# Group norms of a state-space mixer applied to the output products, with two dense tiles and three others moved in the order

## The chip, the cores and the metric

The kernel runs on one core of one Trainium2 chip. The core has a matrix engine (TensorE, PE in the profile; PEld is its weight load), a vector engine (VectorE, DVE), an activation engine (ScalarE, ACT), a general engine (GpSimd, POOL) and a queue engine (SyncE, SP) that issues most transfers. The metric is the device time of one execution in microseconds. Three runs of the kernel before took 1381.81, 1380.92 and 1374.41 us; their median, 1380.92 us, is what the change is measured against.

## What is computed

The reference is one inference step of one decoder layer, for 512 prompt tokens and 64 sampled ones (8 sequences of 8), 576 tokens in all, with a model width of 1024. Everything is fp32.

```
proj = rmsnorm(h) @ w_in                      # columns: z, xbc, dt, rwkv
A: xs, B, C = silu(conv4(xbc));  y = SSD(xs, dt, B, C) + d_skip * xs      # 16 heads x 64, 2 groups
   yg = y * silu(z)
   yg = yg * rsqrt(mean(yg * yg over the 512 channels of a group) + eps)  # per token and group
   y_ssd = yg * ssd_norm
B: y_rwkv = gate * (head_norm(rwkv7(...)) + bonus)                        # 16 heads x 64
h = h + concat(y_ssd, y_rwkv) @ w_out
h = h + (silu(f @ w_gate) * (f @ w_up)) @ w_down,   f = rmsnorm(h, norm_ffn)
h = h + sigmoid(rmsnorm(h) @ w_ple_gate) * (p @ w_ple_proj)
y = rmsnorm(h)
```

The grouped norm has one factor for each token and group of 512 channels. It multiplies a whole column of yg, so it can be applied ahead of the output product, or to that group's share of the product. `ssd_norm` is one factor for each channel and cannot be moved in this way.

## The kernel before

**Layout.** Activations lie transposed, channels on the 128 partitions and the 576 tokens along the row, so a 1024-wide activation is 8 tiles. Each fp32 product is made of three products of halves (hi·hi, hi·lo, lo·hi): `mm3` (L211 to L215) issues them for two stretches of 288 tokens, so one tile of 128 input channels by 128 output channels is 6 matmuls, and `linear` (L217) makes an output tile from a list of input tiles; with 8 input tiles that is 48 matmuls. The weights are streamed: `wsplit` (L189) loads 128x512 of them on SP's queue (raw), makes the high half on ACT (whi, L92 is the one line of all `act` calls) and the low half in turn on POOL and DVE (wlo, L198). `split` (L177, L186) does the same for activations. An output tile lies in PSUM (`lin`, two buffers, until the feed-forward stage opens two more).

**Stages.** Input projections and four quarters of the RWKV mixer come first. A quarter is `prep` (keys bk are made at L560 and L561), `gram` (key-query products by groups of windows, L589, masks at L599), `solve` (triangular inverses by many small DVE operations, L650 and L652), `combine` (L674, L688), `chain` (the serial pass over windows, L765 to L823) and `head_norm` (L875 to L889). Between their steps stand dense tiles from a list: projections of a quarter, convolution tiles (L352, taps at L371, L376 and L377) and gate tiles `zed` (L380), which make silu(z) and park it in memory. The table FP says how many tiles of the list go behind each step of `prep` (entries 0 to 4) and of `gram` (entry 5 behind the first group, 6 behind the third).

After the fourth quarter's chain is written, the string SEQ interleaves what is left: 's' is a step of the state-space generator `ssd` (L968), 'z' a gate tile, 'p' the input-embedding products (`ple_proj`, L947; parked as pp), 'y' loads and splits the first six RWKV result tiles (YR), and 'w' makes the share of those six in the first output tile and parks it (part_d).

The state-space part makes transposes (L1061), chunk states (L1074), eight sampled sequences (L1122) and eight prompt tiles (`prompt`, L1143; its last products are L1170 and L1177, the skip term L1178, the share of earlier chunks L1179). `gated` (L1181) is called for group 0 after prompt tile 5 and for group 1 after tile 7. It multiplies each of four xs tiles by silu(z) (L1190, z read back from memory), adds the squares of the four tiles (ACT, and three additions on POOL, L1196), lets `rstd_by_token` (L302) sum them over channels (20 one-column matmuls, L310), take root and reciprocal (L313) and spread the factors over the partitions (L316), copies them to SBUF (bc), multiplies xs by `ssd_norm` and the factors (DVE, L1204), and splits the result into the halves y (low halves in turn on DVE and POOL, L186).

**Output product.** Seven output tiles take the eight RWKV tiles first (L1244 and after, `residual` adds x at L1261), and later the eight state-space tiles in 48 matmuls, added into h on DVE (L1295); the first tile takes the last two RWKV tiles and the eight state-space tiles in 60 matmuls. After each tile `after` scales h by `norm_ffn` (hg, L1274), splits it for the feed-forward stage (xhi, xlo), squares it and adds the squares up (L1279, mostly on POOL). The 22 feed-forward tiles follow, then `w_down` with the same `after` for the next norm, the embedding gate and the final norm.

**What sets the order.** The program is written in one order; a scheduler then places each engine's instructions by a simulated timeline, with the written order as priority. An instruction that is written later may thus stand earlier if its inputs are there. Each engine runs its own list strictly in order.

Of the kernel before, what the change touches and what calls it, by code (L numbers as in the profile page):

```python
# [8 lines left out]
F32 = mybir.dt.float32  # L9
F32R = mybir.dt.float32r  # L10
# [33 lines left out]
SEQ = "zzszszszspyw"  # L44
# [7 lines left out]
FP = ((1, 0, 1, 0, 1, 0, 0, 0), (1, 0, 1, 0, 1, 0, 0, 0), (1, 0, 1, 0, 1, 0, 0, 0), (0, 0, 0, 0, 0, 0, 0, 3))  # L52
# [22 lines left out]
def hybrid_step(ctx, tc, A):  # L75
# [226 lines left out]
    def rstd_by_token(acc, scale, a=0, b=NT, banks=None):  # L302
# [5 lines left out]
        for i, c in enumerate(ws):  # L308
            for h in (0, 64):
                T.matmul(st[h:h + 64, i:i + 1], acc[:, c + h:c + h + 64], ones[:, 0:1], start=True, stop=True)  # L310
# [657 lines left out]
    def ssd():  # L968
# [174 lines left out]
        def prompt(j):  # L1143
# [35 lines left out]
            G.tensor_tensor(xs[j][:, 192:NT], xs[j][:, 192:NT], er[:], ALU.add)  # L1179

        def gated(g):  # L1181

            qa = mt("bc", [P, NT], bufs=4)
            for i in range(4):
# [6 lines left out]
                if i == 0:  # L1191
                    act(qa[:], xs[j][:], AF.Square)
                else:
                    qb = mt("bc", [P, NT], bufs=4)
                    act(qb[:], xs[j][:], AF.Square)
                    G.tensor_tensor(qa[:], qa[:], qb[:], ALU.add)  # L1196
            std = mt("bc", [P, NT], bufs=4)
            banks = d_ps(), d_ps()
            rstd_by_token(qa, 1.0 / 512, banks=banks)
            act(std[:, 0:448], banks[0][:, 0:448])  # L1200
            act(std[:, 448:NT], banks[1][:, 0:128])
            for i in range(4):
                j = 4 * g + i
                V.scalar_tensor_tensor(xs[j][:], xs[j][:], par("ssd_norm", j), std[:], ALU.mult, ALU.mult)  # L1204
                y2 = k4("y2", [P, 2, NT], dt=F32R)
                split(xs[j][:], None, (None, None), None, lo_eng=(V, G)[i % 2], hi=y2[:, 0], lo=y2[:, 1])
                YS.append((y2[:, 0], y2[:, 1]))

# [11 lines left out]
    YS = []  # L1220
# [45 lines left out]
    for c in range(NPART, 8):  # L1266
        ps = lin_ps()
        linear(YR, ps)
        residual(c, ps, A["xT"][c])

    def after(c, h, gname, pool, tag, bufs, state):

        t = pool.tile([P, NT], F32, tag=tag, name=nm("hg"), bufs=bufs)
        V.tensor_scalar(t[:], h[:], par(gname, c), None, ALU.mult)  # L1274
        state["x"].append(split(t[:], xp, ("xhi", "xlo"), [P, NT]))
# [10 lines left out]

    st = {"x": []}
    for c in range(8):
        ps = lin_ps()
        if c < NPART:  # L1290
            linear(YR[6:8] + YS, ps)
            residual(c, ps, part_d[c][:])
        else:
            linear(YS, ps)
            V.tensor_tensor(hs[c][:], ps, hs[c][:], ALU.add)  # L1295
# [220 lines left out]
```

## Time and profile before

| what | value |
|---|---|
| median of three runs | 1380.92 us (1374.41 to 1381.81) |
| the profiled execution | 1375.24 us |
| its span, first to last instruction | 1373.5 us |
| outside the span | 1.74 us |
| mean granted clock of TensorE | 0.936 |
| PE busy | 1256.6 us (91%) |
| DVE, ACT, POOL busy | 717.5, 576.5, 553.6 us |
| DMA over the span | 97 GB/s |

The stages lie in the trace about as follows: input side and quarters one to three to 530 us, the solve of the fourth quarter 530 to 568, its combine and chain 568 to 672, its head norm 673 to 694, the state-space part 696 to 809, the rest of the output product to 879, then the feed-forward and the last stages.

An execution on the chip was recorded; a row of a timeline is one instruction or a run of like ones: start and duration in us, engine, line of the kernel, operation, output and inputs, shapes, how many, and in brackets the idle time of the engine ahead of it and what ended that. Matmuls overlap, so a matmul's own duration is longer than the distance to the next one, and the distance is its cost. A window's row sums each engine's busy time in a stretch. The granted clock is 1.00 at full speed and 0.50 at half.

### The profile page before, as it was taken

The page shows a single profiled execution, that of the slowest core. Times are in us where ns is not written, and L with a number is a line of the kernel's source. Part 1 is how long each engine was busy: PE and PEld are TensorE (multiplying, and loading weights), DVE is VectorE, ACT ScalarE, POOL GpSimd, SP SyncE. Part 2 cuts the span into 40 slices and gives each one's busy share as a digit, 9 for nine tenths or more (in the row PEclk, how much of TensorE's full clock was granted, in tenths as well). Part 3 has the DMA queues.
Part 4 walks back from the last instruction along what each step waited for, and adds up shares of the span by engine and source line. Part 5 has one row for each costly group of instructions (what it writes and reads, how often), then busy time and mean ns, then how long its engine had stood idle before and what let it go on. Part 6 is the DMA issues. An engine that isn't in the chain of part 4 may idle for free.

```text
span 1373.5 us, 26233 instructions
## 1 busy us (share of the span) xinstructions
PE 1256.6 (91%) x10525; PEld 1158.4 (84%) x10525; DVE 717.5 (52%) x1330; ACT 576.5 (42%) x1148; POOL 553.6 (40%) x547
## 2 busy tenths in 40 slices
PE   6897999999989979888969968999999999999995
PEld 5786897889868858767748858999999999999995
DVE  6648757797778777744365664322222222222265
ACT  6565346534562653433433354333233333222253
POOL 5326415632452253224355665433233233344442
PEclk9997999899979989879969988999999999999998
DMA  4322342234222313432625621322222222222342
GB/s 161 123 70 62 84 119 89 69 99 129 68 73 90 105 63 92 133 134 86 197 83 179 200 69 63 85 77 85 84 79 85 85 79 84 85 80 81 115 133 70
DMA packets 94458, 135.56 MB, mean 99 GB/s; under 512 B 34704, under 2 KB 39056, under 8 KB 94336
## 3 DMA queue, kind: packets, MB, share of 16 engines
q1 hardware_dynamic: 94336, 133.88, 32.0%
q8 instruction: 83, 1.36, 0.4%
q14 instruction: 39, 0.32, 0.1%
HBM read 106.10 MB, written 27.75 MB: 97 GB/s over the span
## 4 chain that ended last, share of the span: by engine, by line
PE 42%; DVE 6%; ACT 2%; DMA 2%; POOL 1%; issue 1%; DVEq 0%; SPq 0%; ACTq 0%; POOLq 0%
PE lin L213 13%; PE lin L215 13%; PE lin L214 13%; DMA raw<-wts 1%; DVE pg L1364 1%; PE d L1127 1%; DVE h L1365 1%; PE d L1139 1%; PE y L1177 0%; DVE xs L1204 0%; DMA yl<-yr_d 0%; ACT sq L92 0%; DVE h L1382 0%; DVE xs L1190 0%; DVE wp L198 0%
## 5 line engine op out<-in xcount | busy, mean ns | idle before, releaser
L213 PE MATMUL lin<-xhi,whi 128*128 128x288 f32 (+1 forms) x1488 | 450.1, 303 | 3.7 <-ACT whi L92 2.2
L215 PE MATMUL lin<-xhi,wlo 128*128 128x288 f32 (+1 forms) x1488 | 447.3, 301 | 2.3 <-POOL wlo L198 2.3
L214 PE MATMUL lin<-xlo,whi 128*128 128x288 f32 (+1 forms) x1488 | 447.4, 301 | 0.6 <-POOL xlo L186 0.6
L198 POOL TENSOR_TENSOR wlo<-raw,whi 128x512 fp32r<-128x512 f32 (+1 forms) x136 | 180.5, 1327 | 490.0 <-ACT whi L92 465.3
L92 ACT ACTIVATE whi<-raw 128x512 fp32r<-128x512 f32 (+1 forms) x272 | 169.0, 621 | 410.1 <-PE lin L214 344.9
L213 PEld LDWEIGHTS lin<-xhi,whi 128*128 128x128 f32 (+1 forms) x1488 | 281.3, 189 | 10.8 <-issue 2.6
L215 PEld LDWEIGHTS lin<-xhi,wlo 128*128 128x128 f32 (+1 forms) x1488 | 281.9, 189 | 8.2 <-POOL wlo L198 3.0
L214 PEld LDWEIGHTS lin<-xlo,whi 128*128 128x128 f32 (+1 forms) x1488 | 281.5, 189 | 5.3 <-issue 1.5
L198 DVE TENSOR_TENSOR wlo<-raw,whi 128x512 fp32r<-128x512 f32 (+1 forms) x136 | 97.1, 714 | 171.8 <-ACT whi L92 169.1
L213 PE MATMUL lin<-ah,whi 128*128 128x288 f32 x352 | 104.1, 296 | 0.0
L215 PE MATMUL lin<-ah,wlo 128*128 128x288 f32 x352 | 103.8, 295 | 0.3
L214 PE MATMUL lin<-al,whi 128*128 128x288 f32 x352 | 103.8, 295 | 0.0
L215 PEld LDWEIGHTS lin<-ah,wlo 128*128 128x128 f32 x352 | 66.3, 188 | 1.0 <-POOL wlo L198 1.0
L214 PEld LDWEIGHTS lin<-al,whi 128*128 128x128 f32 x352 | 66.1, 188 | 0.0
L213 PEld LDWEIGHTS lin<-ah,whi 128*128 128x128 f32 x352 | 66.0, 187 | 0.0
L1323 DVE TENSOR_TENSOR sg<-lin,sg 128x576 f32<-128x576 f32 x22 | 16.7, 758 | 83.2 <-PE lin L215 81.9
L650 DVE TENSOR_TENSOR tmp<-L,Tt 72x30 f32<-72x30 f32 (+14 forms) x120 | 51.6, 430 | 3.2
L1318 DVE TENSOR_TENSOR sg<-lin,rstd 128x576 f32<-128x576 f32 x22 | 16.6, 757 | 68.8 <-PE lin L215 68.7
L213 PE MATMUL lin<-xu,whi 128*128 128x288 f32 x128 | 39.9, 313 | 8.8 <-ACT xu L92 7.1
L215 PE MATMUL lin<-xu,wlo 128*128 128x288 f32 x128 | 39.9, 313 | 7.2 <-DVE wlo L198 5.5
L652 DVE TENSOR_TENSOR Tt<-Tt,tmp 72x30 f32<-72x30 f32 (+14 forms) x120 | 44.3, 369 | 3.4
L186 POOL TENSOR_TENSOR al<-sg,ah 128x576 fp32r<-128x576 f32 x22 | 31.5, 1431 | 32.4 <-ACT ah L92 32.4
(365 smaller groups left out, 2509.4 us busy)
## 6 DMA issues: line engine op xcount, KB each, us to landing
raw<-wts SPq DMA_DIRECT2D x271, 256.0 KB, 2.6
S<-s_wkv SPq DMA_DIRECT2D x8, 512.0 KB, 5.1
hd<-s_ssm SPq DMA_DIRECT2D x8, 512.0 KB, 3.7
o_ssm_s<-hd SPq DMA_DIRECT2D x8, 512.0 KB
xbc_d<-E SPq DMA_DIRECT2D x12, 288.0 KB, 2.1
x<-xT SPq DMA_DIRECT2D x8, 288.0 KB
gate_d<-g SPq DMA_DIRECT2D x8, 288.0 KB, 2.6
bv_d<-rw SPq DMA_DIRECT2D x8, 288.0 KB
```

The costliest lines, as they stand in the source:

```text
L92: S.activation(out, in_, func, bias=bias, scale=scale)
L186: eng.tensor_tensor(lo[:], src, hi[:].bitcast(F32), ALU.subtract)
L198: eng.tensor_tensor(lo[:, 0:n], raw[:, 0:n], hi[:, 0:n].bitcast(F32), ALU.subtract)
L213: T.matmul(ps[:, a:b], whi, xhi[:, a:b], start=first, stop=False)
L214: T.matmul(ps[:, a:b], whi, xlo[:, a:b], start=False, stop=False)
L215: T.matmul(ps[:, a:b], wlo, xhi[:, a:b], start=False, stop=last)
L650: V.tensor_tensor(o, L[:, jx:jx + 1, jx + 1:32].to_broadcast([NB, jx, n]), Tt[:, 0:jx, jx:jx + 1].to_broadcast([NB, jx, n]), ALU.mult)
L652: V.tensor_tensor(Tt[:, 0:jx, jx + 1:32], Tt[:, 0:jx, jx + 1:32], o, ALU.subtract)
L1127: T.matmul(yo[(h % 2) * 64:(h % 2) * 64 + 64, (h // 2) * 8:(h // 2) * 8 + 8], hd[:, h * 64:h * 64 + 64], cd[:, h, b * 8:b * 8 + 8], start= ...
L1139: T.matmul(ps[:], bm[:, i, g * P:g * P + P], xst[:, c], start=i == 0, stop=i == 1)
L1318: V.tensor_tensor(s_[:], ps, rs[:], ALU.mult)
L1323: V.tensor_tensor(s_[:], up, s_[:], ALU.mult)
```

## The change

It has three parts, and no matmul of the dense products is added or taken out.

1. `gated` no longer multiplies by the grouped norm ahead of the split. The high half is made on ACT with the scale `ssd_norm`, the low half on DVE in one operation from xs and the high half. The squares of a group are kept in two tiles (two additions on POOL instead of three), which `rstd_by_token` sums with 20 more one-column matmuls. The factors of each group (bc) are kept in STD. The output product of the state-space tiles is made in two passes over the eight output tiles, one for each group (`scaled`): 24 matmuls, a multiplication of the PSUM tile by the factors on DVE (into yl, two buffers), and an addition into h, on POOL in the first pass and in turn on POOL and DVE in the second. The first output tile's last two RWKV tiles are now 12 matmuls of their own. In `after` the high half comes from ACT with the scale, the low half from one DVE operation, and hg and POOL's low halves are gone, in the feed-forward norm and in the one before the embedding gate. The share of earlier chunks is added on DVE for prompt tiles 6 and 7.
2. SEQ: the first step of the state-space generator now stands ahead of the first two gate tiles, and two gate tiles stand together twice.
3. FP: in quarters one to three the third dense tile stands behind the first group of the key-query products instead of behind `prep`.

The packing of the weights follows the new order, with the same number of loads. Lines of the changed kernel lie 2 to 4 higher up to `gated` (L1177 becomes L1181, L310 L312, L316 L320); `scaled` multiplies at L1297 and adds at L1298, the low half of `after` is L1279, its addition of squares L1284.

```
-SEQ = "zzszszszspyw"
+SEQ = "szzszzszspyw"
...
-FP = ((1, 0, 1, 0, 1, 0, 0, 0), (1, 0, 1, 0, 1, 0, 0, 0), (1, 0, 1, 0, 1, 0, 0, 0), (0, 0, 0, 0, 0, 0, 0, 3))
+FP = ((1, 0, 1, 0, 0, 1, 0, 0), (1, 0, 1, 0, 0, 1, 0, 0), (1, 0, 1, 0, 0, 1, 0, 0), (0, 0, 0, 0, 0, 0, 0, 3))
...
-        for i, c in enumerate(ws):
-            for h in (0, 64):
-                T.matmul(st[h:h + 64, i:i + 1], acc[:, c + h:c + h + 64], ones[:, 0:1], start=True, stop=True)
+        accs = acc if isinstance(acc, tuple) else (acc,)
+        for n, q in enumerate(accs):
+            for i, c in enumerate(ws):
+                for h in (0, 64):
+                    T.matmul(st[h:h + 64, i:i + 1], q[:, c + h:c + h + 64], ones[:, 0:1],
...
-            G.tensor_tensor(xs[j][:, 192:NT], xs[j][:, 192:NT], er[:], ALU.add)
+            (V if j > 5 else G).tensor_tensor(xs[j][:, 192:NT], xs[j][:, 192:NT], er[:], ALU.add)
...
+                q = qb if i else qa
+                act(q[:], xs[j][:], AF.Square)
+                if i in (1, 2):
                     G.tensor_tensor(qa[:], qa[:], qb[:], ALU.add)
...
+                act(hi, xs[j][:], AF.Identity, scale=par("ssd_norm", j))
+                V.scalar_tensor_tensor(lo, xs[j][:], par("ssd_norm", j), hi.bitcast(F32), ALU.mult, ALU.subtract)
+                YS.append((hi, lo))
...
-                V.scalar_tensor_tensor(xs[j][:], xs[j][:], par("ssd_norm", j), std[:], ALU.mult, ALU.mult)
-                y2 = k4("y2", [P, 2, NT], dt=F32R)
-                split(xs[j][:], None, (None, None), None, lo_eng=(V, G)[i % 2], hi=y2[:, 0], lo=y2[:, 1])
-                YS.append((y2[:, 0], y2[:, 1]))
+            STD.append(std)
...
-    for c in range(NPART, 8):
+    for c in range(8):
         ps = lin_ps()
-        linear(YR, ps)
-        residual(c, ps, A["xT"][c])
+        linear(YR if c >= NPART else YR[6:8], ps)
+        residual(c, ps, A["xT"][c] if c >= NPART else part_d[c][:])
...
-        t = pool.tile([P, NT], F32, tag=tag, name=nm("hg"), bufs=bufs)
-        V.tensor_scalar(t[:], h[:], par(gname, c), None, ALU.mult)
-        state["x"].append(split(t[:], xp, ("xhi", "xlo"), [P, NT]))
+        hi, lo = (xp.tile([P, NT], F32R, tag=n, name=nm(n)) for n in ("xhi", "xlo"))
+        act(hi[:], h[:], AF.Identity, scale=par(gname, c))
+        V.scalar_tensor_tensor(lo[:], h[:], par(gname, c), hi[:].bitcast(F32), ALU.mult, ALU.subtract)
+        state["x"].append((hi, lo))
...
+    def scaled(c, g):
+
+        ps = lin_ps()
+        linear(YS[4 * g:4 * g + 4], ps)
+        t = mt("yl", [P, NT], bufs=2)
+        V.tensor_tensor(t[:], ps, STD[g][:], ALU.mult)
+        (V if g and c % 2 else G).tensor_tensor(hs[c][:], hs[c][:], t[:], ALU.add)
+
     st = {"x": []}
     for c in range(8):
-        ps = lin_ps()
-        if c < NPART:
-            linear(YR[6:8] + YS, ps)
-            residual(c, ps, part_d[c][:])
-        else:
-            linear(YS, ps)
-            V.tensor_tensor(hs[c][:], ps, hs[c][:], ALU.add)
+        scaled(c, 0)
+    for c in range(8):
+        scaled(c, 1)
         after(c, hs[c], "norm_ffn", me, "xs", 8, st)
```

27 lines of the change are left out of this document (13 added, 14 removed).

## The prediction

> **What bounds the kernel now.** The head of the page and its row of granted clock come first: how full is the matrix engine, and where is it slowed?
>
> ```profile
> span 1373.5 us, 26233 instructions
> PE 1256.6 (91%) x10525; PEld 1158.4 (84%) x10525; DVE 717.5 (52%) x1330; ACT 576.5 (42%) x1148; POOL 553.6 (40%) x547
> PEclk9997999899979989879969988999999999999998
> ```
>
> PE is busy for 91% of the span, and only about 117 us (1373.5 less 1256.6) are left over. A digit below 9 in the clock row marks slices in which part of the time ran at half clock. What a change can win is therefore read from the places where PE is not full. The table of engine windows, made every 5 us around the end of the state-space part, shows one such place. Its columns are the window, busy us and instruction count for PE, PEld, DVE, ACT and POOL, then the granted clock, the DMA share and GB/s.
>
> ```profile
> 800.00:805.00 5.00, 2.43 (x19) 2.02 (x17) 1.33 (x4) 3.51 (x7) 0.62 (x1) 1.00 0.19 55
> 805.00:810.00 5.00, 4.41 (x27) 3.64 (x27) 4.65 (x4) 3.01 (x7) 3.20 (x3) 0.66 0.00 0
> 810.00:815.00 5.00, 2.61 (x11) 2.61 (x12) 5.00 (x7) 1.18 (x2) 5.00 (x3) 0.76 0.00 0
> 815.00:820.00 5.00, 2.23 (x14) 1.99 (x12) 3.74 (x3) 2.25 (x4) 3.46 (x4) 0.84 0.16 52
> 820.00:825.00 5.00, 2.53 (x25) 2.07 (x25) 0.30 (x2) 1.80 (x4) 1.05 (x1) 0.50 0.00 0
> 825.00:830.00 5.00, 1.99 (x7) 1.67 (x7) 4.23 (x6) 2.73 (x4) 2.77 (x1) 0.50 0.00 0
> 840.00:1340.00 500.00, 499.15 (x3751) 497.39 (x3749) 135.57 (x193) 163.32 (x262) 180.73 (x136) 1.00 0.30 88
> ```
>
> From 800 to 830 PE is about half busy and the clock is down to 0.50, while from 840 to 1340 it is busy for 499.15 of 500 us at clock 1.00. Nothing can be won in the last stretch without taking matmuls out, and the change takes none out. The timeline of PE shows what the waits before 830 are for (start, duration, instruction, and in brackets the idle time and what ended it).
>
> ```profile
> 804.89 2.19 PE L1170 MATMUL d<-bc,hin 128*128 128x128 f32 x12 [2.57 <-ACT bc L92]
> 807.01 1.97 PE L1177 MATMUL y<-sg,xdt 128*64 128x128 f32 x14
> 812.39 0.47 PE L214 MATMUL lin<-y,whi 128*128 128x288 f32 x1 [2.98 <-DVE y L186]
> 821.11 1.23 PE L310 MATMUL d<-ones,bc 128*64 128x1 f32 x20 [3.88 <-POOL bc L1196]
> 823.02 1.30 PE L316 MATMUL d<-ident,rn 128*128 128x128 f32 x5 [0.68 <-DVE rn L313]
> 826.48 0.61 PE L213 MATMUL lin<-y,whi 128*128 128x288 f32 x1 [2.16 <-ACT y L92]
> 828.62 0.61 PE L214 MATMUL lin<-y,whi 128*128 128x288 f32 x1 [1.53 <-DVE y L186]
> 829.27 0.44 PE L213 MATMUL lin<-y,whi 128*128 128x288 f32 x1
> 829.51 0.44 PE L214 MATMUL lin<-y,whi 128*128 128x288 f32 x1
> ```
>
> Each wait is for the chain of the grouped norm: squares added on POOL (L1196), the reciprocal (L313), its spread over partitions (L316), the scaling and the split into y. The last two rows start 0.24 us apart: that is a matmul at half clock. The state-space part ends when the group at 807.01 does, at 808.98. The remaining output products then run until this timeline of DVE, whose L1295 rows follow the last matmul of a tile:
>
> ```profile
> 805.35 5.11 DVE L1204 SCALAR_TENSOR_TENSOR xs<-xs,pv,bc 128x576 f32<-128x576 f32 x4 [4.01 <-ACT bc L92]
> 824.89 3.01 DVE L1204 SCALAR_TENSOR_TENSOR xs<-xs,pv,bc 128x576 f32<-128x576 f32 x4 [2.02 <-ACT bc L92]
> 840.59 0.76 DVE L1295 TENSOR_TENSOR h<-lin,h 128x576 f32<-128x576 f32 x1 [4.12 <-PE lin L215]
> 841.44 0.69 DVE L198 TENSOR_TENSOR wlo<-raw,whi 128x512 fp32r<-128x512 f32 x1
> 846.95 0.76 DVE L1295 TENSOR_TENSOR h<-lin,h 128x576 f32<-128x576 f32 x1 [1.88 <-PE lin L215]
> 878.78 0.76 DVE L1295 TENSOR_TENSOR h<-lin,h 128x576 f32<-128x576 f32 x1 [4.12 <-PE lin L215]
> ```
>
> A tile of 48 matmuls takes 846.95 − 840.59 = 6.36 us, so 0.1325 us a matmul. The last tile ends at 878.78, so the stretch is 878.78 − 808.98 = 69.8 us.
>
> **Part 1: norms on the products.** What PE does after the last state-space matmul, before. 'lin' is an output tile, y the normed halves of a state-space tile, 'd' the norm's small products.
>
> ```order
> L1177 MATMUL y_8562<-sg_8577,xdt_7860 64x128
> L213 MATMUL lin_9122<-y_1321_8508,whi_9125 128x288
> ...
> L310 MATMUL d_8630<-ones,bc_8601 64x1 x10
> L316 MATMUL d_8629<-ident,rn_1350_8641 128x128 x4
> L316 MATMUL d_8630<-ident,rn_1350_8641 128x128
> L213 MATMUL lin_9122<-y_1351_8652,whi_9155 128x288
> ```
>
> The same place on PE in the changed kernel; yh and yl are now the halves of the unnormed y.
>
> ```order
> L1181 MATMUL y_8565<-sg_8580,xdt_7860 64x128
> L213 MATMUL lin_9151<-yh_8482,whi_9154 128x288
> ...
> L312 MATMUL d_8642<-ones,bc_8604 64x1 x10
> ...
> L213 MATMUL lin_9287<-yh_8464,whi_9290 128x288
> L320 MATMUL d_8641<-ident,rn_1350_8663 128x128 x4
> L320 MATMUL d_8642<-ident,rn_1350_8663 128x128
> ```
>
> Before, 24 matmuls of group 0 stand ahead of the norm of group 1 and 24 + 7×48 behind it: 384, or 50.9 us at 0.1325. The other 18.9 us of the 69.8 are waits, the norm's own products and half clock. After, 9 + 15×24 = 369 stand there, because 15 more moved ahead of the end of the state-space part. The norm of group 1 now stands inside group 0's pass, with dense work around it, and group 1's first product comes about 200 matmuls (27 us) behind the end. Its inputs need only two gate products and splits after the end. What remains is 369 × 0.1325 = 48.9 plus 1.23 (L310) plus 1.30 (L316): 51.4 us. **Gain 18.4 us.** The 15 moved matmuls take 2.0 us and stand, with 8 others, where PE waited 2.57 us ahead of 804.89: gain 0.6. If that cover fails, they cost 2.0.
>
> What it costs is on DVE and POOL. In the second pass the rows of DVE are these (L1297 scales a PSUM tile by the norm, L1298 adds it to h, L1279 is the new low half, L198 the weights' low half):
>
> ```order
> L1297 TENSOR_TENSOR yl_9454<-lin_9423,bc_8640 128x576
> L1297 TENSOR_TENSOR yl_9494<-lin_9463,bc_8640 128x576
> L198 TENSOR_TENSOR wlo_9549<-raw_9546,whi_9548 128x512
> L1298 TENSOR_TENSOR h_8757<-h_8757,yl_9494 128x576
> L1279 SCALAR_TENSOR_TENSOR xlo_9458<-h_8692,pv,xhi_9457 128x576
> L1279 SCALAR_TENSOR_TENSOR xlo_9498<-h_8757,pv,xhi_9497 128x576
> L1297 TENSOR_TENSOR yl_9535<-lin_9504,bc_8640 128x576
> ```
>
> Behind a late L1298 or L1279 the next L1297 is late, and with two PSUM tiles the product after the next waits for it. Four L1204 alone took 3.01 us (0.75 each), but 5.11 where POOL was adding beside them. The single-input scaling of h and POOL's operations show the same:
>
> ```profile
> 842.05 0.51 DVE L1274 TENSOR_SCALAR hg<-h,pv 128x576 f32<-128x576 f32 x1
> 847.75 1.45 DVE L1274 TENSOR_SCALAR hg<-h,pv 128x576 f32<-128x576 f32 x1
> 837.26 1.44 POOL L186 TENSOR_TENSOR xlo<-hg,xhi 128x576 fp32r<-128x576 f32 x1 [1.11 <-PE lin L214]
> 847.57 1.31 POOL L198 TENSOR_TENSOR wlo<-raw,whi 128x512 fp32r<-128x512 f32 x1 [3.72 <-ACT whi L92]
> ```
>
> L1295, with one input from PSUM, took 0.76 each time. I therefore let SBUF-only operations of DVE and POOL exclude each other, and L1297 run at 0.76. Per two tiles of the second pass: DVE one add 0.75, two low halves 1.50, one weight half 0.69; POOL one add 1.44, one and a half additions of squares 2.16, one weight half 1.31. The sum is 7.85 us, against 48 × 0.1325 = 6.36 on PE: 1.49 over, 6.0 in four pairs. Some of it can run on beyond the pass, because the feed-forward stage needs the last low half 5.6 us after its start and the squares later still. If all of that slips, the price is 0; if it is paid in full, 6.0; if L1297 (8 × 0.76 = 6.1) is excluded too, 12.1. I take the middle of the first two, **a loss of 3.0**, since the L1295 rows speak against the last. In the first pass a pair has 0.69 + 2×1.44 + 1.31 = 4.88 of 6.36: nothing.
>
> The Trainium skill, page "SBUF — State Buffer", section "Who interferes with whom", says that DVE with two SBUF inputs and a GpSimd instruction that reads SBUF hold one port pair exclusively, and that the second to issue blocks fully. That speaks against this change, and 3.01 against 5.11 agrees. Taken strictly, with no work slipping, the sum below would be 3.0 us less gain.
>
> Removing hg and POOL's low half from the down projection changes nothing: PE is full there (499.15 of 500).
>
> **Part 2: gate tiles (SEQ).** PE before, under the solve of the last quarter; lin is a gate tile, cx the chain of quarter three:
>
> ```order
> L213 MATMUL lin_7028<-xhi_355,whi_7031 128x288
> L788 MATMUL cx_5417<-G_4409,suv_5347 64x64
> L214 MATMUL lin_7028<-xlo_356,whi_7031 128x288
> L215 MATMUL lin_7028<-xhi_355,wlo_7032 128x288
> L797 MATMUL cx_5430<-suv_5347,bkt_5404 64x64 x4
> L788 MATMUL cx_5417<-G_4409,suv_5347 64x64 x3
> ```
>
> and in the changed kernel, the same steps:
>
> ```order
> L792 MATMUL cx_5417<-G_4409,suv_5347 64x64
> L801 MATMUL cx_5430<-suv_5347,bkt_5404 64x64 x4
> L792 MATMUL cx_5417<-G_4409,suv_5347 64x64 x3
> L769 MATMUL cx_5449<-suv_5427,G_4409 128x128 x2
> L777 MATMUL cx_5455<-xs_5452,TT_465 64x64 x4
> ```
>
> Two gate tiles, 96 matmuls (12.7 us), leave this place for the chain of the last quarter; the 96 of the input embedding leave that chain for the head norm; 36 matmuls of the partial output tile go from there to just ahead of the state-space transposes (L1061). The windows of these stages:
>
> ```profile
> 550.00:555.00 5.00, 5.00 (x54) 4.36 (x53) 4.77 (x10) 2.10 (x5) 1.28 (x1) 1.00 0.28 85
> 590.00:595.00 5.00, 3.03 (x32) 2.59 (x31) 2.90 (x8) 3.65 (x7) 0.00 (x0) 0.50 0.96 334
> 660.00:665.00 5.00, 5.00 (x49) 4.77 (x49) 1.12 (x4) 2.60 (x5) 1.29 (x1) 1.00 0.60 194
> 685.00:690.00 5.00, 2.49 (x18) 1.67 (x16) 4.63 (x8) 0.70 (x2) 1.27 (x1) 1.00 0.67 196
> 690.00:720.00 30.00, 20.43 (x118) 13.85 (x119) 19.75 (x28) 10.99 (x22) 19.91 (x16) 0.55 0.18 67
> ```
>
> The solve is bound by DVE (4.77 of 5), so it doesn't get longer without the tiles. The chain keeps its load (96 come, 96 go). The head norm gets 60 more, 8.0 us, and the start of the state-space part 36, at half clock 36 × 0.24 = 8.6. There are waits for most of that: 2.5 of 5 us at 685, 9.6 of 30 at 690. **I take 0.** Below nothing: the two tiles' two weight halves on DVE, 1.4, leave the solve. Above: the partial tile needs YR, which comes over the queue in these rows of the chain of waits; with its order ahead of the transposes, they may wait 3.95 + 2.67 = 6.6 us.
>
> ```profile
> 673.39 3.95 DMA yl<-yr_d
> 679.57 2.67 DMA yl<-yr_d
> ```
>
> **Part 3: the third dense tile (FP).** For quarters two and three it moves behind the first key-query group. These DVE rows (conv tile L371, keys L560) show it for quarter three, and the PE row the wait for keys:
>
> ```profile
> 386.75 0.84 DVE L371 SCALAR_TENSOR_TENSOR h<-E,hw,h 128x600 f32<-128x600 f32 x1
> 392.01 1.51 DVE L560 SCALAR_TENSOR_TENSOR bk<-kk,lo 64x576 f32<-64x576 f32 x2
> 126.64 1.22 PE L589 MATMUL lin<-G,bk 64*128 64x128 f32 x4 [2.71 <-POOL bk L561]
> ```
>
> Three L371 (2.5 us) no longer stand ahead of the keys, in two quarters: at most 5.0 gained. The tile's 48 matmuls now stand between groups: at most 6.4 lost once. Part of either is hidden by the other chains. **I take a gain of 1.0.**
>
> **Sum.** −18.4 − 0.6 + 3.0 + 0 − 1.0 = −17.0 us. The profiled execution took 1375.24 (span plus 1.74 outside), so 1358.2 in its terms; the median is 5.7 higher, 1380.92, and gives **1363.9, say 1364**. A measurement of this kernel can tell about 0.5% (6.9 us) from no change.
>
> **The rivals.** *A, more gain:* the second pass hides its excess (0 for 3.0) and the gram stages win all they can (−5.0 for −1.0): −24.0, 1357. For it speaks that L1295 never stretched; against it, the full DVE and POOL of the second pass. *B, no change:* exclusion takes L1297 too (12.1 for 3.0) and YR holds the transposes for 6.6: −17.0 + 9.1 + 6.6 = −1.3, 1380. For it speaks that most new work goes to the two engines that contend; against it, L1295's constant 0.76. *C, slower:* dense tiles that lost the cover of the solve stand ahead of the serial steps of head norm and state-space start at half clock. All 96 + 36 exposed at 0.24 cost 31.7: +14.7, 1396. It decides from 17.0/0.24 = 71 exposed matmuls on; for it speaks the 0.55 clock at 690, against it the waits that stand there now.
>
> **How the numbers follow.** Forecast 0.54, A 0.22, B 0.15, C 0.09. In the forecast the exclusion at 6.0 leaves −14.0, Part 3 at its worse end (6.4 lost) −9.6, and only both together −6.6, at the bound of 0.5%; so faster is 0.54 + 0.22 = 0.76, same 0.15, slower 0.09. The range reaches from A less the 6.5 us by which the fastest run shown (1374.41) lies below the median, 1350, to B's 1380 and one for rounding, 1381; only C lies outside.
>
> **What would show it.** Right: no PE wait over 1 us and clock 1.00 between the last L1181 and the feed-forward start, some 52 to 58 us apart; the norm's L312 and L320 amid tiles; L1279 and POOL's L1298 stretched beyond 0.75 and 1.44 in the second pass, L1297 at 0.76. Wrong: the tiles of the second pass over 3.9 us each (B), or L1065 behind a wait for YR, and the stages from 600 to 800 longer by more than 7 us (C).

## The result, and the profile after

The changed kernel takes 1393.28 us, the median of five runs (1391.99 to 1395.15), where the kernel before takes 1380.92 (1374.41 to 1381.81). The kernel before has five runs here too, in two groups (1374 to 1376 and 1381 to 1382), so its median says little: the two medians are 12.4 us apart, while the ratio, which uses all runs, is 1.0109, 95% interval 1.0085 to 1.0133. That is slower by about 15 us, where 17 faster was forecast. In the rounds of the experiments the median of the kernel before was 1377.1 to 1377.8; below, a gain or loss in us is the ratio less one, of about 1380.

The head of its page, as before. PE is 91% busy again, in a longer span; its busy time grew by 14.2 us with the same dense products and 40 one-column matmuls more, while the mean granted clock went from 0.936 to 0.931: part of the busy time is matmuls at half clock.

```profile
span 1391.5 us, 26325 instructions
PE 1270.8 (91%) x10565; PEld 1168.9 (84%) x10565; DVE 722.4 (52%) x1333; ACT 577.0 (41%) x1148; POOL 546.8 (39%) x543
```

The timelines of both executions were cut at the same eight events, each the start or end of a row. Lengths in us, from times rounded to 0.1, so that a length can be off by 0.1:

| stretch | before | after | difference |
|---|---|---|---|
| start to the fourth solve | 530.4 | 537.5 | +7.1 |
| fourth solve | 37.6 | 37.7 | +0.1 |
| to the last DVE row of the last head norm (L889) | 125.8 | 126.5 | +0.7 |
| from there to the first state-space row on DVE (L1107, now L1111) | 2.2 | 16.0 | +13.8 |
| to the last state-space matmul (L1177, now L1181) | 113.0 | 114.5 | +1.5 |
| to the first feed-forward row (L1318, now L1327) | 88.3 | 78.9 | −9.4 |
| to the first row of the down projection (L1330, now L1339) | 282.4 | 282.2 | −0.2 |
| to its last row | 124.6 | 127.4 | +2.8 |
| to the end of the span | 69.2 | 70.8 | +1.6 |

They add up to the 18.0 us between the spans. The output product, which the change was about, won 9.4; a stretch of 2 us ahead of the state-space part became 16. Two profiles of one kernel can differ by several us in one stretch (the last section has the figures), so the small differences here mean little.

That stretch on DVE, before: the state-space part starts the moment the last low half of the head norm's result is made on POOL.

```profile
691.96 1.84 DVE L889 SCALAR_TENSOR_TENSOR gb<-gb,pv 128x576 f32<-128x576 f32 x1
696.02 0.68 DVE L1107 TENSOR_TENSOR sg<-d,tk 64x512 f32<-64x512 f32 x1 [2.22 <-POOL xlo L186]
```

And after, where the head norm's last row (L893) ended at 701.7:

```profile
714.77 1.66 DVE L198 TENSOR_TENSOR wlo<-raw,whi 128x256 fp32r<-128x256 f32 x1 [13.03 <-ACT whi L92]
716.36 0.74 DVE L1250 TENSOR_TENSOR pr<-lin,pr 128x576 f32<-128x576 f32 x1
717.73 0.68 DVE L1111 TENSOR_TENSOR sg<-d,tk 64x512 f32<-64x512 f32 x1 [0.63 <-POOL xlo L186]
```

The chain of waits of the changed kernel tells what fills it: the last store of the embedding products (pp), then the loads of the RWKV results (yl), each with its low half on POOL.

```profile
699.61 5.08 DMA pp_d<-pp
705.17 3.05 DMA yl<-yr_d
708.28 1.43 POOL xlo L186
709.72 2.86 DMA yl<-yr_d
...
713.37 2.45 POOL xlo L186 x2
...
716.11 1.60 POOL xlo L186
717.73 0.68 DVE sg L1111
```

The end of POOL's line in that stretch:

```profile
713.37 1.41 POOL L186 TENSOR_TENSOR xlo<-yl,xhi 128x576 fp32r<-128x576 f32 x1 [0.72 <-ACT xhi L92]
714.73 2.97 POOL L186 TENSOR_TENSOR xlo<-gb,xhi 128x576 fp32r<-128x576 f32 x2
```

The last two low halves are made from gb, the head norm's own result, which was there at 701.7. They are late because they stand on POOL behind the six of YR, and those wait for their loads.

L1111 doesn't read xlo. It writes sg, and by the kernel's text sg lies in a pool (mz) that is opened on the same side of the memory when the pools of the stage before (mix) are closed. So the state-space part begins when the last user of the old memory is done. YR's loads and the embedding products' results lie there too: they share three buffers (`cslot`).

The output product, after, on PE. The last state-space group ends at 832.16; PE waits at two places in the 60.2 us to the last scaled tile (L1297 at 892.34).

```profile
831.07 1.09 PE L1181 MATMUL y<-sg,xdt 128*64 128x128 f32 x14
...
838.98 0.37 PE L213 MATMUL lin<-yh,whi 128*128 128x288 f32 x1 [2.27 <-DVE yl L1297]
...
883.47 0.40 PE L213 MATMUL lin<-yh,whi 128*128 128x288 f32 x1 [1.86 <-ACT whi L92]
...
884.69 0.54 PE L215 MATMUL lin<-yh,wlo 128*128 128x288 f32 x1 [0.68 <-POOL wlo L198]
885.02 0.44 PE L213 MATMUL lin<-yh,whi 128*128 128x288 f32 x1
885.26 0.44 PE L214 MATMUL lin<-yl,whi 128*128 128x288 f32 x1
```

The wait at 883.47 is for weights, and behind it PE runs at 0.24 us a matmul. The rows of POOL and ACT say why the weights were late:

```profile
879.55 1.96 POOL L1298 TENSOR_TENSOR h<-h,yl 128x576 f32<-128x576 f32 x1
```

```profile
881.55 0.78 ACT L92 ACTIVATE xhi<-h,pv 128x576 fp32r<-128x576 f32 x1 [2.05 <-POOL h L1298]
882.23 0.67 ACT L92 ACTIVATE hsq<-h 128x576 f32<-128x576 f32 x1
882.81 0.61 ACT L92 ACTIVATE whi<-raw 128x512 fp32r<-128x512 f32 x1
```

POOL's addition took 1.96 us beside DVE's work, where its shortest took 1.42; ACT stood 2.05 us at the high half that needs it; the next tile's weights stood behind that in ACT's line, and PE behind the weights. The stretching is only part of it: this addition and the addition of squares ahead of it on POOL (1.72 us) are together about 0.8 longer than at their shortest, an estimate from these rows. The rest of the 1.86 comes, as far as these rows show, from the order in which POOL and ACT have their work.

### The profile page after: what moved, and what is told of

Read it like the earlier page. It is cut to its first block, busy times and chain, and to the rows that moved or that the text cites. A ratio compares the mean times of both kernels' runs of the same rounds, so it can differ in the third digit from the quotient of the medians.

```text
span 1391.5 us, 26325 instructions
## 1 busy us (share of the span) xinstructions
PE 1270.8 (91%) x10565; PEld 1168.9 (84%) x10565; DVE 722.4 (52%) x1333; ACT 577.0 (41%) x1148; POOL 546.8 (39%) x543
## 4 chain that ended last, share of the span: by engine, by line
PE 52%; DVE 9%; ACT 4%; DMA 3%; POOL 2%; issue 2%; SPq 0%; DVEq 0%; ACTq 0%; POOLq 0%
PE lin L215 14%; PE lin L213 14%; PE lin L214 14%; DMA raw<-wts 1%; POOL wlo L198 1%; ACT L92 1%; PE cx L777 1%; PE d L1143 1%; PE cx L792 1%; PE d L1131 1%; PE cx L769 1%; ACT whi L92 1%; DVE pg L1373 1%; DVE tmp L654 1%; DVE Tt L656 1%
## 5 line engine op out<-in xcount | busy, mean ns | idle before, releaser
L198 POOL TENSOR_TENSOR wlo<-raw,whi 128x512 fp32r<-128x512 f32 x136 | 181.9, 1338 | 497.4 <-ACT whi L92 489.2
L215 PEld LDWEIGHTS lin<-xhi,wlo 128*128 128x128 f32 (+1 forms) x1488 | 285.2, 192 | 11.8 <-POOL wlo L198 4.2
L213 PEld LDWEIGHTS lin<-xhi,whi 128*128 128x128 f32 (+1 forms) x1488 | 284.8, 191 | 11.8 <-ACT whi L92 2.6
L215 PEld LDWEIGHTS lin<-ah,wlo 128*128 128x128 f32 x352 | 66.3, 188 | 3.3 <-POOL wlo L198 2.6
L1327 DVE TENSOR_TENSOR sg<-lin,rstd 128x576 f32<-128x576 f32 x22 | 16.7, 757 | 69.0 <-PE lin L215 68.7
L656 DVE TENSOR_TENSOR Tt<-Tt,tmp 72x30 f32<-72x30 f32 (+14 forms) x120 | 47.6, 397 | 3.2
L593 PE MATMUL lin<-G,bk 64*128 64x128 f32 x288 | 35.9, 363 | 13.1 <-POOL bk L565 8.7
L654 DVE TENSOR_TENSOR tmp<-L,Tt 72x30 f32<-72x30 f32 (+14 forms) x120 | 45.1, 376 | 3.3
```

What stands on the lines that cost most here:

```text
L198: eng.tensor_tensor(lo[:, 0:n], raw[:, 0:n], hi[:, 0:n].bitcast(F32), ALU.subtract)
L213: T.matmul(ps[:, a:b], whi, xhi[:, a:b], start=first, stop=False)
L215: T.matmul(ps[:, a:b], wlo, xhi[:, a:b], start=False, stop=last)
L593: T.matmul(ps[:, c:c + 128].rearrange("p (a t) -> p a t", a=2), s.BK[jj][H[e], g].rearrange("p a t -> p (a t)"), s.G[H[e], g, jj, :, e], s ...
L654: V.tensor_tensor(o, L[:, jx:jx + 1, jx + 1:32].to_broadcast([NB, jx, n]), Tt[:, 0:jx, jx:jx + 1].to_broadcast([NB, jx, n]), ALU.mult)
L656: V.tensor_tensor(Tt[:, 0:jx, jx + 1:32], Tt[:, 0:jx, jx + 1:32], o, ALU.subtract)
```

## The experiments

All were timed in three rounds against the kernel before. Each gives the ratio with its interval, and the stretches of the table that tell, in us; "gap" is the one from the head norm to the state-space part, "down" the down projection.

| kernel | ratio (95%) | 4th solve starts | gap | state space | to feed-forward | down |
|---|---|---|---|---|---|---|
| before | | 530.4 | 2.2 | 113.0 | 88.3 | 124.6 |
| the change | 1.0109 (1.0085 to 1.0133) | 537.5 | 16.0 | 114.5 | 78.9 | 127.4 |
| norm alone | 0.9966 (0.9942 to 0.9990) | 537.2 | 2.2 | 118.2 | 73.1 | 127.1 |
| gate-tile order alone | 1.0088 (1.0062 to 1.0114) | 530.0 | 15.8 | 108.6 | 87.7 | 124.6 |
| dense tile alone | 1.0083 (1.0056 to 1.0109) | 537.6 | 2.2 | 117.0 | 88.9 | 124.6 |
| norm and dense tile | 1.0007 (0.9983 to 1.0031) | 537.8 | 2.2 | 118.7 | 73.7 | 127.1 |
| norm and gate-tile order | 1.0056 (1.0030 to 1.0081) | 534.9 | 14.9 | 114.5 | 74.9 | 127.2 |
| change, YR first | 1.0087 (1.0061 to 1.0113) | 537.6 | 12.0 | 115.2 | 75.1 | 127.2 |
| change, no partial tile | 1.0061 (1.0030 to 1.0091) | 538.0 | 14.7 | 116.3 | 76.5 | 123.7 |
| change, more YR buffers | 1.0073 (1.0048 to 1.0099) | 534.9 | 4.9 | 115.4 | 75.1 | 127.0 |
| norm, PSUM addition | 0.9955 (0.9935 to 0.9975) | 534.9 | 2.2 | 118.8 | 70.0 | 127.3 |
| norm, turn kept | 0.9958 (0.9927 to 0.9989) | 530.7 | 2.3 | 116.9 | 73.4 | 125.3 |
| norm, old after | 0.9973 (0.9948 to 0.9998) | 530.1 | 2.3 | 114.7 | 81.2 | 124.6 |
| norm, PSUM addition, turn kept | 0.9903 (0.9869 to 0.9936) | 534.0 | 2.2 | 113.6 | 66.3 | 125.2 |
| dense tile, two quarters | 1.0041 (1.0021 to 1.0061) | 536.8 | 2.2 | 116.2 | 84.3 | 124.6 |
| third dense tile taken out | 1.0027 (1.0010 to 1.0044) | 542.3 | 2.2 | 113.3 | 88.3 | 124.7 |

An interval is 2 to 5 us to either side. Those of the three kernels that work on the gap overlap with the change's, so their gains over the change are less sure than their stretches.

**The three parts by themselves.** The norm alone is the change with both tables set back:

```
-SEQ = "szzszzszspyw"
+SEQ = "zzszszszspyw"
-FP = ((1, 0, 1, 0, 0, 1, 0, 0), (1, 0, 1, 0, 0, 1, 0, 0), (1, 0, 1, 0, 0, 1, 0, 0), (0, 0, 0, 0, 0, 0, 0, 3))
+FP = ((1, 0, 1, 0, 1, 0, 0, 0), (1, 0, 1, 0, 1, 0, 0, 0), (1, 0, 1, 0, 1, 0, 0, 0), (0, 0, 0, 0, 0, 0, 0, 3))
```

> Only the norm on the products (two passes, new low halves), with the order tables of before. Theory (the gate-tile order is what loses, by the late partial tile ahead of the state-space start): 6 us faster than before, made of 10.5 gained between the end of the state-space part and the feed-forward start and 4.5 lost in the down projection and after it. Rival (the two passes lose, because DVE and POOL hold each other up): 5 us slower or more, with the state-space part itself longer.

Faster by 4.7 us (0.34%): the theory's size. In the profile the output product won 15.2 where the theory had 10.5, the down projection lost 2.5 and what follows 2.7. The state-space part was 5.2 longer, but kernels with the very same instructions there differ by 5 (the last section).

The order of gate tiles on the kernel before is the one line `SEQ = "szzszzszspyw"`:

> Only the new order of gate tiles and state-space steps on the kernel before. Theory: 14 us slower, all of it between the last head norm and the first state-space products, with the 36-matmul partial tile and its wait for the RWKV loads ahead of the transposes; the solve 3 to 5 us shorter. Rival (the norm loses): within 3 us of before.

Slower by 12 us. The place is right, the gap grew from 2.2 to 15.8, but the solve was not shorter (37.5 against 37.6), so that detail of the theory fell. The profiled execution, 1383.59, is the fastest of its seven (median 1391.74), so its stretches show less than the ratio.

The dense tile on the kernel before is the FP line of the change:

> Only the third dense tile moved behind the first key-query group. Theory: 5 us slower, built up in the key-query stages of quarters two and three. Rival (it is worth the 1 us gain of the prediction): 1 us faster, at most 5.

Slower by 11 us: more than the theory said, and against the prediction's gain. The key-query products of quarter three, first and last rows of L589 on PE, before:

```profile
378.03 0.48 PE L589 MATMUL lin<-G,bk 64*128 64x128 f32 x2
...
405.64 1.16 PE L589 MATMUL lin<-G,bk 64*128 64x128 f32 x16
```

and with the tile between them:

```profile
379.60 0.79 PE L589 MATMUL lin<-G,bk 64*128 64x128 f32 x2 [2.69 <-POOL bk L561]
...
411.87 1.16 PE L589 MATMUL lin<-G,bk 64*128 64x128 f32 x16 [0.43 <-ACT G L92]
```

From 28 to 32 us between these starts, and the stage began 1.6 us later. In the first two quarters the stages went from 24 to 28 and 29 us, and they began only 4 and 2 us sooner. The tile is not hidden there.

The pair of norm and dense tile (SEQ set back) and the pair of norm and gate-tile order (FP set back):

> The whole change without the new gate-tile order. Theory: 1 us faster than before (6 gained by the norm, 5 lost by the dense tile), and 12 to 15 us faster than the changed kernel. Rival (the gate-tile order is not the cause): as slow as the changed kernel, 10 us or more over before.

> The changed kernel with the dense tile's old place: norm and gate-tile order together. If the shares add up: 7 us slower than before (5 won by the norm, 12 lost by the order), 8 faster than the changed kernel. If the tile's place is worth its 11 us here as it is alone: 4 slower than before. If only the 6 that it cost beside the norm: 9 slower.

The first is 1 us slower than before (0.07%, an interval that takes in no change), 14 faster than the change. The second is 7.7 slower: norm and gate-tile order add up (−4.7 + 12.1 = 7.4). The dense tile cost 11 alone, 6 beside the norm and 7 beside both; the intervals of these overlap, and a share of 7 to 8 would fit all three.

**The gap.** YR's loads ahead of the embedding products, `SEQ = "szzszzszsypw"`:

> The changed kernel with the loads of the RWKV results (YR) ahead of the input-embedding products instead of behind them; the partial tile still stands ahead of the state-space transposes on PE, and its addition ahead of the first state-space operations on DVE. Theory (what costs at the start of the state-space part is the wait for these loads behind the stores of the embedding products): 6 to 9 us faster than the changed kernel, so 5 to 9 us slower than before, the DVE wait of 13 us at this place down to under 6. Rival (it is the 36 matmuls themselves that stand in the way): within 2 us of the changed kernel, 13 to 17 over before.

Three us faster than the change, by ratio: between the two. The gap is 12.0. DVE at its end:

```profile
714.39 0.76 DVE L1250 TENSOR_TENSOR pr<-lin,pr 128x576 f32<-128x576 f32 x1 [1.77 <-PE lin L215]
715.07 0.67 DVE L1111 TENSOR_TENSOR sg<-d,tk 64x512 f32<-64x512 f32 x1
```

L1111 no longer waits for POOL; it stands behind the partial tile's addition, and that waits for PE. POOL's low halves of gb had waited until 708.72 for PE as well. So once the loads are early, the dense matmuls of the embedding products and the partial tile stand in the way, and the rival has its share. Next, no partial tile, `SEQ = "szzszzszspy"`:

> The changed kernel without the partial tile (no 'w'): the first output tile takes its eight RWKV tiles like the others, so nothing of it stands ahead of the transposes, and 36 dense matmuls (4.8 us) come later. Theory (the partial tile and its wait): 7 to 10 us faster than the changed kernel, 5 to 8 over before, with the state-space part starting 12 us earlier. Rival (the loads hold the state-space part up anyway, or the two gate tiles are what costs): within 2 us of the changed kernel.

About 7 us faster than the change in all, but not at the place: the gap is 14.7, and the state-space part started at 717.6 as in the change. The theory that the partial tile stands in the way falls, with the loads at this place; what the kernel won, it won elsewhere. The down projection is 123.7; POOL and DVE have changed places there in their turn at the weights' low halves. DVE and POOL of this kernel:

```profile
702.03 0.82 DVE L893 SCALAR_TENSOR_TENSOR gb<-gb,pv 128x576 f32<-128x576 f32 x1
717.63 0.68 DVE L1111 TENSOR_TENSOR sg<-d,tk 64x512 f32<-64x512 f32 x1 [14.78 <-POOL xlo L186]
```

```profile
713.49 1.40 POOL L186 TENSOR_TENSOR xlo<-yl,xhi 128x576 fp32r<-128x576 f32 x1 [0.81 <-ACT xhi L92]
714.85 2.75 POOL L186 TENSOR_TENSOR xlo<-gb,xhi 128x576 fp32r<-128x576 f32 x2
```

With nothing else between them, L1111 waits 14.78 us for POOL's last low half of the old stage, that of gb behind those of YR. So the third of this group changes only how fast those loads and halves go through: two more buffers, and the low halves in turn on two engines.

```
-                t = cslot("yl")
+                t = cslot("yl") if j % 3 else sp.tile([P, NT], F32, tag="vo", name=nm("yl"), bufs=2)
                 nc.sync.dma_start(t[:], yr_d[j][:])
-                YR.append(split(t[:], xp, ("xhi", "xlo"), [P, NT], lo_eng=G))
+                YR.append(split(t[:], xp, ("xhi", "xlo"), [P, NT], lo_eng=(V, G)[j % 2]))
```

> The changed kernel with two more buffers for the loads of the RWKV results, and their low halves in turn on DVE and POOL. Theory (the first state-space operations write buffers that lie where the stage before had its own, so they start when the last low half of that stage is made, and that is late because the loads stand behind the embedding products' stores for the same three buffers): the state-space part starts 6 to 9 us earlier, and the kernel is 5 to 8 us faster than the changed one, 6 to 10 over before. Rival (the dense matmuls of the moved tiles set the start): no earlier start, within 2 us of the changed kernel.

The state-space part starts at 708.6 instead of 717.7, and the kernel is 5 us faster than the change: the theory. The dense matmuls of the moved tiles are all still there. The gap is 4.9 instead of 16.0; the stretch from the solve to the end of the head norm got about 4.5 longer (DVE now makes low halves in it, 700.17 and 703.59), and the fourth solve started 2.6 sooner. Its first state-space row still waits for POOL's last low half:

```profile
708.59 0.68 DVE L1111 TENSOR_TENSOR sg<-d,tk 64x512 f32<-64x512 f32 x1 [0.61 <-POOL xlo L186]
```

**The dense tile.** Its new place in quarters one and two alone, and the tile in none of the entries of quarters one to three (`(1, 0, 1, 0, 0, 0, 0, 0)`):

> Only the dense tile's new place, and only in quarters one and two; quarter three as before. Theory (each key-query stage gets 4.5 to 5 us longer by the tile and only part of that is won back ahead of it; quarter three loses most, 5 of the 7 us): 1 to 5 us slower than before, the fourth solve starting 1 to 3 us later. Rival (the loss comes from the first two and is carried on): 9 to 11 us slower like the edit in all three.

Slower by 5.6 us (1.0041, 1.0021 to 1.0061): about half of what all three cost, and between theory and rival. The fourth solve started 6.4 us later, not 1 to 3.

> The kernel before with the third dense tile of quarters one to three taken out of preparation and key-query products, so that it comes with the next tiles, under the solve. Theory (the tile costs in the key-query stage because PE, on whose line the products stand, has no room of that size there, 48 matmuls against waits of 2 to 3 us): the stages shorter than the 24, 24 and 28.5 us of before or equal, each solve starting 3 to 6 us earlier, and what is won there lost later where the tile is made, within 7 us of before. Rival (the stage is late because the convolution's vector operations stand in the line of DVE): stages as long as with the tile.

1.0027 (1.0010 to 1.0044), 3.7 us slower, as expected in all; the profiled execution (1385.41) is the slowest of its ten. The first stage took 22.1 us and the first solve started 5 us earlier; the third took 26.0. The second took 27.5, against the theory, and the later solves started 4, 12 and 12 us later; that this is because the next quarter's own tiles come later in the list was not tried. Whether the tile costs by its matmuls or by its vector operations stays open.

**The second pass and the step behind it.** The product scaled in PSUM and added from there by DVE, and for the other kernel one line in `after`:

```
-        t = mt("yl", [P, NT], bufs=2)
-        V.tensor_tensor(t[:], ps, STD[g][:], ALU.mult)
-        (V if g and c % 2 else G).tensor_tensor(hs[c][:], hs[c][:], t[:], ALU.add)
+        V.tensor_tensor(ps, ps, STD[g][:], ALU.mult)
+        V.tensor_tensor(hs[c][:], ps, hs[c][:], ALU.add)
...
         state["x"].append((hi, lo))
+        flip[0] += 1
```

> The norm on the products alone (order tables of before), but the product is scaled in place in PSUM and added to h by DVE from there; POOL adds only squares. Theory (DVE and POOL exclude each other on operations that use SBUF alone, and the waits of the second pass come from that): 4 to 6 us faster than the norm alone with its additions from SBUF, so 8 to 11 us faster than before. Rival (the second pass is late because the PSUM tiles or the activation engine's line are late): within 2 us of the norm alone, 3 to 6 faster than before, or slower than it since the PSUM tile is held 0.8 us longer.

> The norm on the products alone, with the turn of the two engines that make low halves advanced once in each call of after, as the split there did before. Theory (the down projection and the embedding gate lose 5 us because without that turn POOL makes the same loads of every tile): 4 to 5 us faster than the norm alone, 8 to 10 faster than before, the down projection at 17.8 us a tile again. Rival (they lose by the longer low halves on DVE): within 1 us of the norm alone.

6.2 us faster than before with the PSUM addition, 5.8 with the turn kept, against 4.7 of the norm alone: 1 to 1.5 us each, less than either theory said and inside the intervals. The profiles show both at their places: 70.0 instead of 73.1 to the feed-forward stage, and 125.3 instead of 127.1 in the down projection. The old form of `after` (hg, then `split`), the lines that the change removed there:

> The norm on the products with the old scaling and split behind each output tile (hg on DVE, low halves in turn on POOL and DVE), order tables of before. Theory (the new form of that step costs 2.5 us in the down projection, by the turn of the low halves, and 2.7 us behind it): the down projection back at 124.6 us from its first to its last tile and the end 65 us behind, so up to 5 us faster than the norm alone if the second pass loses nothing by it. Rival (the old form adds so much to POOL in the second pass that it loses there what it wins later): the same time as the norm alone, the output product 4 to 5 us longer.

The down projection is back at 124.6, and the output product takes 81.2, 8 longer: the rival, and more than its 4 to 5. As fast as the norm alone. And both single edits together:

> The norm on the products with the addition from PSUM and with the turn of the low halves advanced in after, order tables of before. If the two single edits (1.5 and 1 us) add up: 7 us faster than before. Rival (they are within what a run varies by): 4 to 5, like the norm alone.

1364.33 us (1364.20 to 1365.62), ratio 0.9903, 0.9869 to 0.9936: 13.4 us faster than before. It beats both kernels. The parts promise 7.3; that it is more than their sum is not shown, since the intervals of the four kernels together leave room for that difference. Its windows show PE full at full clock through the second pass, and its rows that DVE and POOL still stretch each other (1.26 for 0.68, 1.80 for 1.30) without PE waiting over 0.6 us at any place of the output product:

```profile
850.00:860.00 10.00, 9.71 (x73) 9.46 (x72) 7.18 (x9) 5.17 (x10) 8.03 (x7) 1.00 0.25 79
860.00:870.00 10.00, 9.93 (x74) 9.60 (x73) 7.28 (x9) 5.32 (x9) 5.55 (x4) 1.00 0.26 80
```

```profile
865.68 0.76 DVE L1297 TENSOR_TENSOR lin<-lin,bc 128x576 f32<-128x576 f32 x1
866.34 1.26 DVE L198 TENSOR_TENSOR wlo<-raw,whi 128x512 fp32r<-128x512 f32 x1
```

```profile
862.77 1.80 POOL L198 TENSOR_TENSOR wlo<-raw,whi 128x512 fp32r<-128x512 f32 x1
```

The changed kernel's window at the same place was 7.46 busy at a clock of 0.83:

```profile
880.00:890.00 10.00, 7.46 (x43) 6.99 (x42) 8.15 (x7) 3.85 (x6) 8.11 (x5) 0.83 0.22 54
```

Keeping the turn gives every weight half of the second pass but the last to POOL (in the change, in turn), and that leaves DVE its line for the tiles; what this is worth was not separated from the turn's effect on the down projection.

The pair of PE waits at the weights, 1.86 and 0.68 us in the change, stands in all seven kernels that add the scaled tiles from SBUF, with the new `after` and the partial tile (1.8 to 2.3 and 0.7). The kernel without the partial tile, in which POOL and DVE have changed places in the turn, has a single wait of 0.7 us there; the two kernels that add from PSUM have none over 0.6. As far as these kernels tell, the pair of waits comes with the additions from SBUF, and another turn can leave it (turn kept, 2.3 and 0.7) or take it away; how much of it is the stretching and how much the place in the engines' lines was not separated.

## Why the prediction was wrong

The forecast was 17 faster, the result 15 slower. Of the 32 us between them, by the ratios, about 12 are from Part 2, 8 from Part 3 (7.3 lost beside the other two, 1.0 forecast as gained) and 11 from Part 1 (16.0 forecast, 4.7 won alone).

**Part 2 failed, in the step "There are waits for most of that … I take 0".** It asked where the moved matmuls find room on PE. They found it: the clock was 1.00 from 685 to 705, and the stretch up to the end of the head norm is only 0.7 us longer. What decided was what stands behind these matmuls. With the tiles ahead of them the embedding products ran late, in the head norm; their stores, then the loads of YR, then the low halves on POOL came later with them, and the next stage cannot begin before they are done, since its buffers lie in theirs. The prediction had both rows of yl and the bound of 6.6 us, but put it at the transposes behind the partial tile, and counted two loads where six go through three buffers. It cost 13.8 in the profile and 12 by the runs. The wait behind POOL's xlo stood in the trace of before (2.22 at 696.02), at a row that does not read xlo.

**Part 3 had the wrong sign.** "A gain of 1.0" took the room in the key-query stage for waits; the stages grew by 4 to 5 us and what stood ahead of them shrank by less. It also counted two quarters, and a loss of the tile once; the table FP moves the tile in three, and all three stages grew (24.1 to 28.3, 24.0 to 29.2, 28.5 to 33.2). Share: 6 to 11 us.

**Part 1 was right in its raw gain, wrong in what it costs elsewhere.** Forecast for the stretch to the last output tile was 18.4 gained and 3.0 lost, so 51.4 + 3.0 = 54.4 us. With the norm alone it is 875.16 − 820.82 = 54.3, as forecast. In the change it is 60.2, so the term "a loss of 3.0" is 8.8 there: 4.8 us are the three waits shown, and 24 matmuls at 0.24 instead of 0.133 behind them make about 2.6 more. The change is the worst case here: the other kernels with this second pass need 54.7 to 56.5, and with another FP the scheduler can put the instructions of these stages in another order, as it did between the norm alone and the norm with the dense tile. The working of the 51.4 us held: the kernel with both edits needs 865.68 − 813.35 = 52.3.

The stretching of DVE and POOL is there as read (L1298 1.96 for 1.42, L1204 1.92 for 0.81, L1297 0.74 to 0.76 always), as the Trainium skill's page "SBUF — State Buffer", section "Who interferes with whom", has it. But the way to PE was another: L1297 was late only once, at 838.98, and that in the first pass, which the prediction put at "nothing"; DVE still had the gate products and low halves of the second group in its line there. The larger wait came through ACT, which stands in order with the weights behind a high half that waits for POOL. The prediction counted two engines' sums and left out the third that stands between.

What is missing in the norm alone, 11 us, is not in that stretch. The down projection and what follows it account for 5 of them, as below; the gain of 0.6 ahead of the last state-space products cannot be read among differences of 5 us between like executions, and the rest was not located.

**"Changes nothing" for the down projection was wrong.** It takes 2.8 us more. `split` also hands the next low half to the other engine; without it a tile has six turns instead of seven, and the same loads of each tile fall to the slower one. First and last rows of the stage, before and after:

```profile
1179.66 0.76 DVE L1330 TENSOR_TENSOR dn<-lin,rstd 128x576 f32<-128x576 f32 x1 [0.33 <-PE lin L215]
1304.30 0.76 DVE L1330 TENSOR_TENSOR dn<-lin,rstd 128x576 f32<-128x576 f32 x1 [3.28 <-PE lin L215]
```

```profile
1193.34 0.76 DVE L1339 TENSOR_TENSOR dn<-lin,rstd 128x576 f32<-128x576 f32 x1 [4.06 <-PE lin L215]
...
1320.70 0.74 DVE L1339 TENSOR_TENSOR dn<-lin,rstd 128x576 f32<-128x576 f32 x1
```

Keeping the turn took about 2 of it back, and the kernel without the partial tile, where DVE and POOL have changed places in a turn of six, is at 123.7: it matters which loads fall to which engine. The 1.6 to 3.9 us behind the down projection in all kernels with the norm on the products were not traced to a cause; the gate-tile order alone has 1.8 there as well.

**The rivals.** C came within 3 us of the time, and its price was of something else: 132 matmuls exposed at half clock, of which the 96 of the embedding products ran in the head norm, all but about a dozen at full clock. What it had right is that tiles which lose the solve's cover delay the start of the state-space part; that it came so near is luck. B had the wait for YR, half as large, and exclusion where L1297 is not excluded.

## What to carry to other kernels

Look in the trace of before for a wait whose releaser is no input of the waiting row: a buffer may change hands there, and then every instruction that uses the old memory, a store and a load too, stands ahead of the next stage, however much room the engines have. When two engines get slower beside each other, follow what each result releases on a third, in-order engine, since that is where the weights of the next tile may stand. A helper that deals work out in turn passes an edit on to every later stage that uses it. And before a difference between two profiles is explained, look at what executions of the same instructions differ by in that stretch.

## What was not expected of the hardware

A short wait was enough for half clock: behind 1.86 and 0.68 us of waiting at 883.47 and 884.69 the matmuls ran 0.24 us apart until 888, and behind the 2.27 us at 838.98 they did so from 840.58 to 842.98.

Executions with the same instructions up to there reached the fourth solve between 530.0 us (gate-tile order alone) and 537.2 (norm alone), and kernels of the new dense-tile place reached it between 534.9 and 538.0. The state-space part, too, took from 113.6 to 118.8 us in the five kernels that have the norm and the old order tables, and in these every engine has the same instructions there in the same order. What differs is the granted clock. The second 10 us of the state-space part, with the norm alone and in the fastest kernel:

```profile
712.59:722.59 10.00, 8.64 (x69) 5.78 (x71) 4.56 (x8) 2.26 (x5) 5.29 (x6) 0.55 0.14 54
```

```profile
709.70:719.70 10.00, 8.65 (x92) 6.17 (x93) 4.89 (x9) 3.02 (x7) 5.44 (x7) 0.83 0.14 54
```

PE is busy alike, at a clock of 0.55 and 0.83, and gets through 69 and 92 matmuls. Why the clock rose sooner in one was not found. Of the 12.7 us by which the fastest kernel's span is shorter than that of the norm alone, 3.2 lie ahead of the fourth solve and 4.6 in the state-space part, where both run the same instructions; whether the four runs of the fastest kernel, all within 1.5 us, were fast by that too stays open. Shares below some 5 us are therefore read from the ratios, not from two profiles.
